# Queries and keys produced feature-major, with their rotary halves swapped by transfers inside SBUF

## The chip, the core and the metric

One decoder layer runs on one core of a Trainium2 chip. The metric is the device time of one execution in microseconds. The kernel before takes 363.92 us (median of three runs, 363.71 to 363.99); the execution that was profiled took 363.52 us, of which 361.7 us is the span from its first to its last instruction.

## What is computed

The layer has 256 positions and width 1024. All products are made in float32 accuracy by splitting each operand into a high and a low part that the matrix engine takes ("h" and "l"), and adding three products: high by high, high by low, low by high.

```
proj  = x @ w_in          # [q 512 | k 512 | v 512 | B 512 | C 512 | h 512 | gates 2048]
q, k  = rotate the first 16 of each head's 64 dimensions   (8 heads)
y_att = softmax(mask(q @ k.T / 8)) @ v @ w_attn_out         # one block of 256 keys, causal
y_cnv = (B * causal_dwconv3(C * h)) @ w_conv_out
mix   = (sigmoid(g_att) * y_att + sigmoid(g_cnv) * y_cnv) @ w_o
x     = LayerNorm(alpha * x + mix)
u     = causal_dwconv3(x @ w_up);  f = (silu(u_gate) * u_val) @ w_down
x     = LayerNorm(alpha * x + f)
```

The rotation takes, per head, dimensions 0 to 7 as x1 and 8 to 15 as x2 and gives x1*cos - x2*sin and x2*cos + x1*sin. The angle is the position times one of eight frequencies.

## The kernel before, in words

The schedule is written out by hand: each engine executes its instructions in the order in which the program issues them. `plan()` cuts all weights into chunks of at most 128 x 2048 numbers, which SP loads in order into three `raw` buffers (`issue_dma`). Each chunk holds units; a unit is split into a high part (`wh`, ScalarE copies with rounding) and a low part (`wl`, VectorE subtracts). There are nine buffers of each. A chunk's buffer is free for the next load when VectorE has made the low part of its last unit.

**The x stage (lines 571 to 629).** Chunks 0 to 7 each hold one block of 128 features of x, transposed, and the rows of `w_in` that belong to it: 512 columns of q, 512 of k, 512 of v. For each block k, `qkv_passes` issues for q, k and v and for each half t of the positions three matmuls of 512 columns (line 596): x is the stationary operand, the weights stream past, and the result is position-major (128 positions by 512 features). Six accumulators collect it over eight blocks: four for q and k in the pool `acc`, two for v in the pool `ps`. The pools have four banks each, taken in rotation. `rope_tables` makes the cosines and sines position-major, 8 numbers per position, in three parts after blocks 2, 3 and 4.

**The stage C0 (lines 545 to 720).** From unit `C0` on, units are made in pairs by `two_units` and `cols_pair`: here the weights are stationary and x streams past, so the result is feature-major (128 features by 256 positions). A *wide* matmul (line 338) streams the high and the low part of x together, 512 columns; a *narrow* one (line 345) streams the high part alone past the low part of the weights, 256 columns. One unit takes 8 of each, over 8 blocks. Order within a pair: 8 wide of the first unit, 8 wide of the second, 8 narrow of the first, 8 narrow of the second. The pairs come as h0, c0, b0, h1, c1, b1 (two halves of h, C and B), then eight pairs of gates g. Each pair takes two `acc` banks, so pair b0 takes over the banks of h0, which VectorE frees with `conv_sum_dve` (line 642).

What else happens in this stage is hung on units by `at(unit, engine part, function)` and issued by `slot(u)`: first the unit's matmuls, then the hung matrix and ScalarE work, then splits of weights four to five units ahead, then hung VectorE work. `rope(t)` (lines 372 to 375, VectorE) rotates q and k position-major at C0 and C0 + 1; `qk_transpose` (line 383) turns them feature-major by 16 matrix-engine transposes at C0 + 2, behind the first unit of pair c0; `qk_h` and `qk_l` (lines 390, 393, 228) split the result into `qkT`. `scores` (line 411) is hung at C0 + 4 for head pairs 0 and 1, and at C0 + 9 for 2 and 3: 20 small matmuls each, behind the first unit of b0 and the second of c1. Masks, softmax, transposes of the probabilities and the products with v follow at later units.

GpSimd has little to do: constants at the start, 128 x 256 additions of masks (line 419) and of outputs, and the loads of the norm parameters.

Of the kernel before, what the change touches and what calls it, by code (L numbers as in the profile page):

```python
# [8 lines left out]
F32 = mybir.dt.float32  # L9
# [6 lines left out]
P = 128  # L16
# [35 lines left out]
PIECES = {0: (0, 768, 1280, 1792), 1: (0, 768, 1792)}  # L52
# [3 lines left out]
LAST = 4  # L56


def plan():
# [80 lines left out]
def layer_kernel(ctx: ExitStack, tc: tile.TileContext, x, wpack, cpack, ln1_g, ln1_b, ln2_g, ln2_b, out):  # L140
# [28 lines left out]
    XR_CHUNK = 20  # L169
# [78 lines left out]

    mask = cst.tile([P, 384], F32, name="mask")
# [14 lines left out]
    invf = cst.tile([P, 8], F32, name="invf")  # L264
    for i, f in enumerate(INV_FREQ):
        nc.gpsimd.memset(invf[:, i:i + 1], f)


    consts = cst.tile([P, 162], F32, name="consts")
    nc.sync.dma_start(consts, cpack)  # L270
    posi = consts[:, 160:162].bitcast(I32)
# [15 lines left out]
    cs = cst.tile([P, 2, 2, 8], F32, name="cs")  # L287

    RT = {}

    def rope_tables(part):

        if part == 2:
            nc.scalar.activation(cs, RT["r"], AF.Sin)
            return
        parts = two_pi_parts(6, 4)
        if part == 1:
            n, r = RT["n"], RT["r"]
            for c in parts[1:]:
                nc.vector.scalar_tensor_tensor(r, n, -c, r, op0=ALU.mult, op1=ALU.add)  # L300
            nc.vector.tensor_scalar(r[:, 0], r[:, 0], math.pi / 2, None, op0=ALU.add)
            nc.vector.tensor_scalar(r, r, PI_LO, -PI_LO, op0=ALU.min, op1=ALU.max)
            return
        posf = cst.tile([P, 2], F32, name="posf")
        nc.vector.tensor_copy(posf, posi)
        ang = cst.tile([P, 2, 8], F32, name="ang")
        nc.vector.tensor_tensor(ang, posf[:, :, None].to_broadcast([P, 2, 8]),
                                invf[:, None, :].to_broadcast([P, 2, 8]), op=ALU.mult)
        n = RT["n"] = cst.tile([P, 2, 2, 8], F32, name="nrev")
        r = RT["r"] = cst.tile([P, 2, 2, 8], F32, name="rrem")  # L310
        for f, ph in ((0, 0.25), (1, 0.0)):
            nc.vector.tensor_scalar(n[:, f], ang, 1.0 / TWO_PI, ph, op0=ALU.mult, op1=ALU.add)
        nc.vector.tensor_scalar(n, n, MAGIC, MAGIC, op0=ALU.add, op1=ALU.subtract)
        for f in range(2):
            nc.vector.scalar_tensor_tensor(r[:, f], n[:, f], -parts[0], ang, op0=ALU.mult, op1=ALU.add)
# [41 lines left out]
    qk = big.tile([P, 2, 2, AW], F32, tag="rows", name="qk")  # L357
# [5 lines left out]
    aT = big.tile([P, 4, 2, S], F32R, tag="d8", name="aT")  # L363
    yT = big.tile([P, 4, 2, S], F32R, tag="e8", name="yT")

    def rope(t):
        xv = qk[:, t].rearrange("p a (h d) -> p (a h) d", d=HD)[:, :, 0:16].rearrange("p h (i f) -> p h i f", i=2)
        a = scratch([P, 16, 2, 8], f"ra{t}")
        b = scratch([P, 16, 2, 8], f"rb{t}")
        co = cs[:, 0, t][:, None, None, :].to_broadcast([P, 16, 2, 8])  # L370
        si = cs[:, 1, t][:, None, None, :].to_broadcast([P, 16, 2, 8])
        nc.vector.tensor_tensor(a, xv, co, op=ALU.mult)
        nc.vector.tensor_tensor(b, xv, si, op=ALU.mult)
        nc.vector.tensor_tensor(xv[:, :, 0, :], a[:, :, 0, :], b[:, :, 1, :], op=ALU.subtract)
        nc.vector.tensor_tensor(xv[:, :, 1, :], a[:, :, 1, :], b[:, :, 0, :], op=ALU.add)

    def qk_transpose(g2):

        b = ps_bank(f"qkt{g2}")
        for gi in range(2):  # L380
            g = 2 * g2 + gi
            for t in range(2):
                nc.tensor.transpose(b[:, gi * 256 + t * P:gi * 256 + (t + 1) * P],
                                    qk[:, t, g // 4, (g % 4) * P:(g % 4 + 1) * P], ident)
        QB[g2] = b.rearrange("p (g t) -> p g t", g=2)
# [3 lines left out]
    def qk_h(g2):  # L389
        nc.scalar.activation(qkT[:, 0, 2 * g2:2 * g2 + 2, :], QB[g2], AF.Copy)  # L390

    def qk_l(g2):
        low(qkT[:, 1, 2 * g2:2 * g2 + 2, :], QB[g2], qkT[:, 0, 2 * g2:2 * g2 + 2, :])
# [3 lines left out]
    def scores(ps):  # L397
# [4 lines left out]
        for t in range(2):  # L402
            n = (t + 1) * P
            for p in ps:
                for a, b in ((0, slice(0, 2)), (1, 0)) if t == 0 else ((0, 0), (0, 1), (1, 0)):
                    for j in range(2):
# [4 lines left out]
                        nc.tensor.matmul(o, qkT[hs, a, p, t * P:(t + 1) * P], qkT[hs, b, 4 + p, 0:n],  # L411
# [81 lines left out]
    def attend_h(p):  # L493
        nc.scalar.activation(aT[:, p, 0, :], PR[p, "c"][:, 0], AF.Copy)
# [40 lines left out]
    def evac_rows(i, banks):  # L535
        for t in range(2):
            nc.scalar.activation(qk[:, t, i, :], banks[t], AF.Copy)

# [6 lines left out]
    C0 = U[(OFF_H, 0)]  # L545
    for t in range(2):
        at(C0 + t, "dve", rope, t)
    for g2 in (0, 2, 1, 3):
        at(C0 + 2, "pe", qk_transpose, g2)
        at(C0 + 3, "act", qk_h, g2)  # L550
        at(C0 + 3, "dve", qk_l, g2)

# [53 lines left out]
    for p in (0, 2):  # L606
        qkv_passes(0, 0, (0, 1), (p,))
# [535 lines left out]
```

## Time and profile before

| what | value |
|---|---|
| median of three runs | 363.92 us |
| the profiled execution | 363.52 us |
| its span | 361.7 us |
| granted TensorE clock, mean | 0.999 |
| moved by DMA | 69.63 MB, 193 GB/s over the span |

In the profile, PE is the matrix engine's matmuls and PEld its weight loads, DVE is VectorE, ACT ScalarE, POOL GpSimd, SP the queue that issues the weight loads. A timeline row gives the start, the length, the engine, the line, the output and inputs, the tile shapes, the count of instructions merged into the row, and in brackets the idle time before it with what ended that. Matmuls overlap, since the next one streams in while the last one drains. So the length of a single matmul is no price; the distance from one start to the next is.

### The profile page before, as it was taken

The page shows a single profiled execution, that of the slowest core. Times are in us where ns is not written, and L with a number is a line of the kernel's source. Part 1 is how long each engine was busy: PE and PEld are TensorE (multiplying, and loading weights), DVE is VectorE, ACT ScalarE, POOL GpSimd, SP SyncE. Part 2 cuts the span into 40 slices and gives each one's busy share as a digit, 9 for nine tenths or more (in the row PEclk, how much of TensorE's full clock was granted, in tenths as well). Part 3 has the DMA queues.
Part 4 walks back from the last instruction along what each step waited for, and adds up shares of the span by engine and source line. Part 5 has one row for each costly group of instructions (what it writes and reads, how often), then busy time and mean ns, then how long its engine had stood idle before and what let it go on. Part 6 is the DMA issues. An engine that isn't in the chain of part 4 may idle for free.

```text
span 361.7 us, 5228 instructions
## 1 busy us (share of the span) xinstructions
PE 355.0 (98%) x1935; PEld 307.0 (85%) x1935; DVE 298.5 (83%) x518; ACT 232.2 (64%) x415; POOL 21.7 (6%) x49
## 2 busy tenths in 40 slices
PE   9999999999999999999999999999999999999993
PEld 8888888888898888888888888888888888888883
DVE  4696887989795969989769888969779697999875
ACT  5576758787977966653357576656757476577800
POOL 2000001000000113301000000000000000000110
PEclk9999999999999999999999999999999999999999
DMA  7988563536653454688160845456281736663011
GB/s 287 337 298 331 169 234 117 216 116 222 245 208 142 134 216 130 250 318 290 61 234 18 332 131 219 146 202 226 125 342 40 316 102 247 232 235 116 3 51 65
DMA packets 11098, 69.63 MB, mean 193 GB/s; under 512 B 1216, under 2 KB 1472, under 8 KB 4032
## 3 DMA queue, kind: packets, MB, share of 16 engines
q1 hardware_dynamic: 10352, 67.00, 50.7%
q0 software_dynamic: 576, 2.10, 1.9%
q8 instruction: 15, 0.25, 0.3%
q10 hardware_dynamic: 144, 0.20, 0.1%
q14 instruction: 11, 0.09, 0.1%
HBM read 68.24 MB, written 1.05 MB: 192 GB/s over the span
## 4 chain that ended last, share of the span: by engine, by line
PE 95%; issue 3%; DVE 1%; POOLq 0%; POOL 0%; DVEq 0%
PE pb L338 20%; PE pb L345 11%; PE g L338 8%; PE d L320 5%; PE d L321 5%; PE d L322 4%; PE g L345 4%; PE y L338 4%; PE q L596 3%; PE k L596 3%; PE v L596 3%; PE b L338 2%; PE y L345 2%; PE c L338 2%; PE o L320 2%
## 5 line engine op out<-in xcount | busy, mean ns | idle before, releaser
L209 DVE TENSOR_TENSOR wl<-raw,wh 128x1024 fp32r<-128x1024 f32 x99 | 121.9, 1233 | 22.1 <-ACT wh L199 21.5
L199 ACT ACTIVATE wh<-raw 128x1024 fp32r<-128x1024 f32 x99 | 103.7, 1054 | 25.9 <-DMA raw<-in_wpack 25.8
L338 PE MATMUL pb<-x1T,wh 128*128 128x512 f32 x320 | 76.2, 390 | 0.0
L338 PEld LDWEIGHTS pb<-x1T,wh 128*128 128x128 f32 x320 | 59.7, 188 | 12.1
L345 PEld LDWEIGHTS pb<-x1T,wl 128*128 128x128 f32 x320 | 41.0, 191 | 1.6
L345 PE MATMUL pb<-x1T,wl 128*128 128x256 f32 x320 | 41.5, 283 | 0.0
L232 DVE TENSOR_TENSOR wl<-raw,wh 128x1024 fp32r<-128x1024 f32 (+1 forms) x29 | 27.3, 982 | 6.1 <-ACT wh L231 5.8
L338 PE MATMUL g<-xT,wh 128*128 128x512 f32 x128 | 31.8, 395 | 0.0
L320 PE MATMUL d<-wh,f 128*128 128x512 f32 x76 | 29.8, 392 | 0.0
L321 PE MATMUL d<-wl,f 128*128 128x512 f32 x76 | 29.8, 391 | 0.0
L322 PE MATMUL d<-wh,f 128*128 128x512 f32 x76 | 29.6, 389 | 0.0
L231 ACT ACTIVATE wh<-raw 128x1024 fp32r<-128x1024 f32 (+1 forms) x29 | 23.7, 859 | 8.1 <-PE o L322 4.0
L338 PEld LDWEIGHTS g<-xT,wh 128*128 128x128 f32 x128 | 23.2, 188 | 4.6
L863 ACT ACTIVATE fb<-pb 128x512 f32<-128x512 f32 x20 | 11.9, 593 | 17.5 <-PE pb L345 17.4
L881 DVE SCALAR_TENSOR_TENSOR fc<-fb,consts,fc 128x254 f32<-128x254 f32 x40 | 19.3, 483 | 1.4
L879 DVE SCALAR_TENSOR_TENSOR fc<-fb,consts,fc 128x255 f32<-128x255 f32 x40 | 19.1, 478 | 0.0
L873 ACT ACTIVATE fc<-fb,consts 128x256 f32<-128x256 f32 x40 | 18.0, 497 | 1.2 <-DVE fb L867 1.1
L345 PEld LDWEIGHTS g<-xT,wl 128*128 128x128 f32 x128 | 16.4, 191 | 0.7
L322 PEld LDWEIGHTS d<-wh,f 128*128 128x128 f32 x76 | 14.3, 188 | 3.1
L345 PE MATMUL g<-xT,wl 128*128 128x256 f32 x128 | 16.6, 282 | 0.0
L320 PEld LDWEIGHTS d<-wh,f 128*128 128x128 f32 x76 | 14.3, 189 | 2.6
L321 PEld LDWEIGHTS d<-wl,f 128*128 128x128 f32 x76 | 14.3, 189 | 2.4
(206 smaller groups left out, 593.8 us busy)
## 6 DMA issues: line engine op xcount, KB each, us to landing
raw<-in_wpack SPq DMA_DIRECT2D x55, 1024.0 KB, 4.9
raw<-in_wpack SPq DMA_DIRECT2D x6, 896.0 KB, 6.6
xr<-in_x SPq DMA_DIRECT2D x1, 1024.0 KB, 7.1
ln<-in_ln_g POOLq DMA_DIRECT2D x2, 512.0 KB, 5.2
ln<-in_ln_b POOLq DMA_DIRECT2D x2, 512.0 KB, 5.8
raw<-in_wpack SPq DMA_DIRECT2D x2, 384.0 KB, 3.9
raw<-in_wpack SPq DMA_DIRECT2D x2, 256.0 KB, 3.5
raw<-in_wpack SPq DMA_DIRECT2D x1, 512.0 KB, 5.6
```

Source lines behind the costliest of these rows:

```text
L199: nc.scalar.activation(units[u]["h"], raw_of(u), AF.Copy)
L209: nc.vector.tensor_tensor(units[u]["l"], raw_of(u), units[u]["h"].bitcast(F32), op=ALU.subtract)
L231: nc.scalar.activation(h, src, AF.Copy)
L232: (eng or nc.vector).tensor_tensor(l, src, h.bitcast(F32), op=ALU.subtract)
L320: nc.tensor.matmul(o, ah, bh, start=start, stop=False)
L321: nc.tensor.matmul(o, ah, bl, start=False, stop=False)
L322: nc.tensor.matmul(o, al, bh, start=False, stop=stop)
L338: nc.tensor.matmul(bank, un["h"][:, k, n0:n0 + P], b[:, k].rearrange("p a s -> p (a s)"), start=k == 0, stop=False)
L345: nc.tensor.matmul(bank[:, 0:S], un["l"][:, k, n0:n0 + P], b[:, k, 0], start=False, stop=k == nk - 1)
L596: nc.tensor.matmul(banks[m][t], (xl if p == 2 else xh)[:, k, t * P:(t + 1) * P], wl if p == 1 else wh, start=k == 0 and p == 0, stop=k == ...
L879: nc.vector.scalar_tensor_tensor(c[:, 1:S], pb[:, a * S:a * S + S - 1], w_ffn(1, j), c[:, 1:S], op0=ALU.mult, op1=ALU.add)
L881: nc.vector.scalar_tensor_tensor(c[:, 2:S], pb[:, a * S:a * S + S - 2], w_ffn(0, j), c[:, 2:S], op0=ALU.mult, op1=ALU.add)
```

## The change

- The q and k weights become eight units of 128 columns, in the order q0 k0 q1 k1 q2 k2 q3 k3. Six of them (`QK = 6`) stand beside v in each chunk of the x stage, which shrinks from 1792 to 1536 columns; the last two (q3, k3) come as an own chunk of two units, at the new mark `qk`, ahead of C0, and are made by `two_units` like every other pair.
- In the x stage, per block: v as before (6 matmuls of 512), then for the six q/k units one wide and one narrow matmul each. v comes first, except in the last block, where it comes last.
- `qk_act` and `qk_dve` add the two halves of each feature-major result into `qk`, as the h, C and B units do. `qk_swap` copies, per group of 64 partitions, eight partitions of `qk` into `swap` by transfers inside SBUF, four transfers of 8 partitions x 1024 numbers for units 0 to 3 and four for units 4 to 7, on SP's queue.
- The rotation is cos * q on VectorE (`rope_cos`), sin * swapped on GpSimd (`rope_sin`), and their sum on VectorE (`rope_sum`), over whole 128 x 512 tiles in which unrotated dimensions have cosine 1 and sine 0. `qk_h` and `qk_l` split the sum from SBUF, not from a PSUM bank.
- The cosines and sines are feature-major, 128 x 256 each. Frequencies come out of a constant tile by one more matrix-engine transpose at the start; positions come by a transfer of their own (`prow`, on GpSimd's queue); the tables are made in five parts after blocks 1 to 5.
- `qk_transpose` and its 16 transposes are gone.
- The two lines that hang `scores` at C0 + 4 and C0 + 9 stand twice in the new text.

```diff
@@ plan
     for k in range(KT):
         chunk((1, S, [("xT", k, k + 1, 0, S)]),
-              (2, 512, [("w_in", k, k + 1, 0, 1024)]),
-              (1, 512, [("w_in", k, k + 1, 1024, 1536)]))
+              (1, AW, [("w_in", k, k + 1, 2 * AW, 3 * AW)]),
+              (QK, P, [("w_in", k, k + 1, qk_col(s), qk_col(s) + P) for s in range(QK)]))
+    mark("qk")
+    chunk(*[(8, P, [("w_in", 0, 8, qk_col(s), qk_col(s) + P)]) for s in (QK, QK + 1)])
@@ constants
+    freqs = tmp.tile([P, P], F32, tag="gs", name="freqs", bufs=3)
+    nc.gpsimd.memset(freqs, 0.0)
+    for h, sign in enumerate((-1.0, 1.0)):
+        for i, f in enumerate(INV_FREQ):
+            nc.gpsimd.memset(freqs.rearrange("p (j d) -> p j d", j=2)[:, :, 8 * h + i:8 * h + i + 1], sign * f)
+    nc.tensor.transpose(warm[:, P:2 * P], freqs, ident)
+    posr = cst.tile([P, S], I32, name="posr")
+    nc.gpsimd.dma_start(posr, bass.AP(tensor=prow.tensor, offset=prow.offset, ap=[[0, P], [1, S]]))
@@ rope_tables, on 128 x 256 tiles
+        if part == 0:
...
+            nc.vector.tensor_copy(posf, posr)
+            nc.vector.tensor_scalar(r, posf, freq[:, 0:1], None, op0=ALU.mult)
+            nc.vector.tensor_scalar(n, r, 1.0 / TWO_PI, None, op0=ALU.mult)
+            nc.vector.tensor_scalar(n, n, MAGIC, MAGIC, op0=ALU.add, op1=ALU.subtract)
+        if part in (0, 1, 2):
+            for c in (parts[0:1], parts[1:4], parts[4:])[part]:
+                nc.vector.scalar_tensor_tensor(r, n, -c, r, op0=ALU.mult, op1=ALU.add)
+        if part == 2:
             nc.vector.tensor_scalar(r, r, PI_LO, -PI_LO, op0=ALU.min, op1=ALU.max)
+        if part == 3:
+            nc.vector.scalar_tensor_tensor(a, r, -1.0, r, op0=ALU.mult, op1=ALU.max)
+            nc.scalar.activation(cs[:, 1], r, AF.Sin)
+            nc.scalar.activation(cs[:, 0], a, AF.Sin, bias=halfpi, scale=-1.0)
+        if part == 4:
+            nc.vector.tensor_scalar(cs[:, 0], cs[:, 0], freq[:, 2:3], freq[:, 1:2], op0=ALU.mult, op1=ALU.add)
+            nc.vector.tensor_scalar(cs[:, 1], cs[:, 1], freq[:, 2:3], None, op0=ALU.mult)
@@ the rotation
+    def qk_act(s, bank):
+        QB[s] = scratch([P, S], f"qb{s}", tag="gs", bufs=3)
+        nc.scalar.activation(QB[s], bank()[:, S:2 * S], AF.Copy)
+    def qk_dve(s, bank):
+        nc.vector.tensor_tensor(qk[:, s], bank()[:, 0:S], QB[s], op=ALU.add)
+    def qk_swap(b):
+        for p in range(0, P, HD):
+            for h in (0, 8):
+                nc.sync.dma_start(swap[p + h:p + h + 8, 4 * b:4 * b + 4], qk[p + 8 - h:p + 16 - h, 4 * b:4 * b + 4])
+    def rope_cos(p):
+        QB["r", p] = scratch([P, 2, S], f"rope{p}")
+        nc.vector.tensor_tensor(QB["r", p], qk[:, 2 * p:2 * p + 2], table(0), op=ALU.mult)
+    def rope_sin(p):
+        nc.gpsimd.tensor_tensor(swap[:, 2 * p:2 * p + 2], swap[:, 2 * p:2 * p + 2], table(1), op=ALU.mult)
+    def rope_sum(p):
+        nc.vector.tensor_tensor(QB["r", p], QB["r", p], swap[:, 2 * p:2 * p + 2], op=ALU.add)
@@ what is hung where
+    S0, C0 = U["qk"], U[(OFF_H, 0)]
+    for p in range(2):
+        at(S0, "dve", rope_cos, p)
+        at(S0, "dve", rope_sin, p)
+        at(S0 + 1, "dve", rope_sum, p)
+        at(C0 + p, "act", qk_act, QK + p, lambda p=p: q3k3[p])
+        at(C0 + p, "dve", qk_dve, QK + p, lambda p=p: q3k3[p])
+    at(C0 + 1, "dve", qk_swap, 1)
+    for p in range(4):
+        if p > 1:
+            at(C0 + p - 1, "dve", rope_cos, p)
+            at(C0 + 2, "dve", rope_sin, p)
+            at(C0 + 3, "dve", rope_sum, p)
+        at(C0 + p // 2 * 4, "act", qk_h, p)
+        at(C0 + p // 2 * 4, "dve", qk_l, p)
+    at(C0 + 4, "pe", scores, (0, 1))
+    at(C0 + 9, "pe", scores, (2, 3))
 
     at(C0 + 4, "pe", scores, (0, 1))
     at(C0 + 9, "pe", scores, (2, 3))
@@ the x stage
+    def qk_passes(k, ss):
+        w = units[U["qkv"] + 3 * k + 2]
+        for s in ss:
+            nc.tensor.matmul(qb[s], w["h"][:, s, :], xT[:, k].rearrange("p a s -> p (a s)"), start=k == 0, stop=False)
+        for s in ss:
+            nc.tensor.matmul(qb[s][:, 0:S], w["l"][:, s, :], xh[:, k], start=False, stop=k == KT - 1)
...
+    q3k3 = two_units(S0, ("q3", "k3"))
```

More of the change, by code (lines that the diff above doesn't have):

```diff
@@ L304, in rope_tables @@
[L304 to L312, printed above, removed]
@@ L377, in qk_transpose @@
[L377 to L385, printed above, removed]
-    QB = {}
[L389 to L393, printed above, removed]
+    QB = {}
@@ L395, in layer_kernel, with qk_l @@
+    def qk_l(p):
+        low(qkT[:, 1, 2 * p:2 * p + 2, :], QB["r", p], qkT[:, 0, 2 * p:2 * p + 2, :])
     SB, SM, PR = {}, {}, {}
@@ L606, in layer_kernel @@
     for p in (0, 2):
-        qkv_passes(0, 0, (0, 1), (p,))
+        v_passes(0, (p,))
     nc.vector.tensor_tensor(wl0[:, 0], w0[:, 0], wh0[:, 0].bitcast(F32), op=ALU.subtract)
-    qkv_passes(0, 0, (0, 1), (1,))
-    split_part(1, 1, 2)
-    qkv_passes(0, 1, (0, 1), (0, 2, 1))
-    split(2)
-    qkv_passes(0, 2, (0, 1), (0, 2, 1))
+    v_passes(0, (1,))
+    split_start(2)
+    for s in (0, 3):
+        split_part(2, s, s + 3)
+        qk_passes(0, range(s, s + 3))
+    rope_freqs()
     qkv_split(1)
```

137 lines of the change are left out of this document (64 added, 73 removed).

## The prediction

> **What bounds the kernel now.** I read the engines' busy times first, then the chain that ended last, then who waits for whom with the filter on the matrix engine.
>
> ```profile
> span 361.7 us, 5228 instructions
> PE 355.0 (98%) x1935; PEld 307.0 (85%) x1935; DVE 298.5 (83%) x518; ACT 232.2 (64%) x415; POOL 21.7 (6%) x49
> PE 95%; issue 3%; DVE 1%; POOLq 0%; POOL 0%; DVEq 0%
> PE warm L245 <- PEq L1133: 0.8, 1, 0.8
> ```
>
> The busy 98% alone proves little, since overlapping matmuls count as busy. The last row does: in the whole span the matmuls wait for nothing but the start of the program. So a matmul added or removed moves the end by its distance to the next one, and any wait that the change puts in front of a matmul is added whole. The question is thus twofold: how much matmul work comes and goes, and whether VectorE, 83% busy, still keeps ahead. The timeline of the matrix engine gives the prices, as distances between starts:
>
> ```profile
> 4.43 1.75 PE L596 MATMUL q<-wh,xT 128*128 128x512 f32 x4
> ...
> 9.21 0.39 PE L596 MATMUL q<-wh,xT 128*128 128x512 f32 x1
> ...
> 33.69 0.39 PE L596 MATMUL q<-wh,xT 128*128 128x512 f32 x1
> ...
> 37.77 3.79 PE L338 MATMUL h<-xT,wh 128*128 128x512 f32 x16
> 41.40 2.08 PE L345 MATMUL h<-xT,wl 128*128 128x256 f32 x16
> 43.31 2.01 PE L338 MATMUL c<-xT,wh 128*128 128x512 f32 x8
> 45.16 1.91 PE L383 MATMUL qkt<-ident,qk 128*128 128x128 f32 x16
> 46.83 2.07 PE L338 MATMUL c<-xT,wh 128*128 128x512 f32 x8
> 48.74 2.08 PE L345 MATMUL c<-xT,wl 128*128 128x256 f32 x16
> 50.65 2.00 PE L338 MATMUL b<-xT,wh 128*128 128x512 f32 x8
> 52.58 1.43 PE L411 MATMUL s<-qkT 64*128 64x256 f32 x20
> 53.95 2.09 PE L338 MATMUL b<-xT,wh 128*128 128x512 f32 x8
> 55.88 2.08 PE L345 MATMUL b<-xT,wl 128*128 128x256 f32 x16
> 57.79 3.82 PE L338 MATMUL h<-xT,wh 128*128 128x512 f32 x16
> ...
> 69.01 1.44 PE L411 MATMUL s<-qkT 64*128 64x256 f32 x20
> 70.38 3.96 PE L338 MATMUL b<-xT,wh 128*128 128x512 f32 x16
> ```
>
> A wide matmul costs (41.40 - 37.77)/16 = 0.227 us, a narrow one (43.31 - 41.40)/16 = 0.119, a clean pair of units 5.54. Block 0 of the x stage takes 4.78 us for 18 matmuls, 0.70 more than 18 x 0.227; the later blocks 4.08 each.
>
> **The change on the matrix engine.** q and k now: 2 x 2 x 3 x 8 = 96 matmuls of 512 columns, 96 x 0.227 = 21.8 us. After: 8 units x 8 blocks, 64 wide and 64 narrow, 14.5 + 7.6 = 22.2. The columns are the same, but a narrow matmul costs more than half a wide one: **+0.4**. v is unchanged.
>
> The 16 transposes go. Pair c takes 50.65 - 43.31 = 7.34 against 5.54 for h, so their worth, with the change of mode around them, is **-1.8** (between -1.7, their own distance 46.83 - 45.16, and -1.8).
>
> The scores double. The new text hangs both calls twice, and nothing takes the first copy out, so 40 small matmuls come on top, each burst right behind its twin. A burst lasts 53.95 - 52.58 = 1.37, and 70.38 - 69.01 = 1.37: **+2.7**. Bounds: by columns alone, 16 x 256 + 4 x 128 shared between two halves of the array, 2304 at 0.227/512, 1.02 a burst, 2.0 in all; above, pair b's full excess, 57.79 - 50.65 - 5.54 = 1.60, twice: 3.2. I take 1.37, since a twin needs no change of mode.
>
> The transpose of the frequencies stands behind the warm-up, ahead of the first block. GpSimd's 17 small fills are done near 2 us, and the first block waits for data until 4.43; it costs nothing, or 0.1 (a transpose's distance) without that cover.
>
> Sum: 0.4 - 1.8 + 2.7 = **+1.3** (0.6 to 1.8).
>
> **The x stage.** A block now asks 6 x 0.227 + 6 x 0.346 = 3.44 us of the matrix engine, not 4.08; its end comes at 4.43 + 0.70 + 8 x 3.44 = 32.65. Can VectorE follow?
>
> ```profile
> 18.24 1.83 DVE L232 TENSOR_TENSOR wl<-raw,wh 128x1024 fp32r<-128x1024 f32 x2 [0.52 <-ACT wh L231]
> 19.98 0.16 DVE L305 CAST posf<-consts 128x2 f32<-128x2 int32 x1
> ...
> 21.14 0.42 DVE L232 TENSOR_TENSOR xT<-raw,xT 128x256 fp32r<-128x256 f32 x1
> ...
> 23.23 1.32 DVE L300 SCALAR_TENSOR_TENSOR rrem<-nrev,rrem 128x32 f32<-128x32 f32 x6
> ...
> 24.89 0.42 DVE L232 TENSOR_TENSOR xT<-raw,xT 128x256 fp32r<-128x256 f32 x1
> ...
> 64.24 1.01 DVE L450 TENSOR_SCALAR sm<-sm,st 128x128 f32<-128x128 f32 x4
> ...
> 66.96 1.92 DVE L658 SCALAR_TENSOR_TENSOR ct<-z,consts,ct 128x256 f32<-128x256 f32 x4
> ...
> 26.67 0.42 ACT L231 ACTIVATE xT<-raw 128x256 fp32r<-128x256 f32 x1 [0.67 <-DMA raw<-in_wpack]
> raw<-in_wpack SPq DMA_DIRECT2D x6, 896.0 KB, 6.6
> ```
>
> The tables cost 1.16 + 1.66 = 2.8 us now (19.98 to 21.14, 23.23 to 24.89). Over 128 x 256 a fused operation takes 1.92/4 = 0.48 and a simple one about 0.3; with some 0.05 where each waits for the last, the five parts are 1.9, 1.6, 1.95, 0.5 and 0.7, **6.6 together**. A block's low parts take about 1.8 (1536 columns in 1.83 now). So three blocks ask 3.4 to 3.75 of VectorE against 3.44. What covers this is its lead: the last block's data lands at 26.67 and is used at 33.69. After, its use comes at 29.2. Smaller chunks land sooner (I take 24.1, from 6.0 us of landing after the release of the buffer, a little under the 6.6 for larger ones), and through VectorE's queue its low parts are ready near 29.1. The lead is used up, no more: 0, bound 2.
>
> **The stage behind it.** With q3/k3 the pairs start at 32.65 (S0), 38.19 (h0), 43.73 (c0) and 49.27 (b0). Pair b0 needs h0's two banks, which VectorE empties.
>
> ```profile
> 39.77 1.23 DVE L209 TENSOR_TENSOR wl<-raw,wh 128x1024 fp32r<-128x1024 f32 x1
> 40.91 0.42 DVE L372 TENSOR_TENSOR ra<-qk,cs 128x256 f32<-128x256 f32 x1
> ...
> 42.11 1.22 DVE L209 TENSOR_TENSOR wl<-raw,wh 128x1024 fp32r<-128x1024 f32 x1
> ...
> 45.58 0.41 DVE L642 TENSOR_TENSOR ch<-h,ch 128x256 f32<-128x256 f32 x1
> 45.91 1.21 DVE L209 TENSOR_TENSOR wl<-raw,wh 128x1024 fp32r<-128x1024 f32 x1
> 47.05 2.47 DVE L228 TENSOR_TENSOR qkT<-qkt,qkT 128x512 fp32r<-128x512 f32 x4
> 49.44 0.41 DVE L642 TENSOR_TENSOR ch<-h,ch 128x256 f32<-128x256 f32 x1
> 55.77 0.74 POOL L419 TENSOR_TENSOR lo<-lo,mask 128x256 f32<-128x256 f32 x1 [0.74 <-ACT lo L418]
> ...
> 56.03 1.56 DVE L209 TENSOR_TENSOR wl<-raw,wh 128x1024 fp32r<-128x1024 f32 x1
> ...
> 0.74 2.27 SPq L177 DMA_DIRECT2D raw<-in_wpack  x5
> out<-x SPq DMA_DIRECT2D x2, 256.0 KB, 2.0
> ```
>
> Now the banks come free at 46 and 50, some 4 us before 50.65 and 53.95. In their place: rotation goes from 2 x 1.2 us (40.91 to 42.11) to eight sums of 0.34, four products and four sums of 0.62 (2.47/4, an operation of that size), 7.7 us, while qkT's lows stay 2.5. Add the tables' 3.8 and VectorE has **9 us more** before pair h1, and only 4 of lead.
>
> Hence its queue, from 29.1: last table part 0.7; four splits of 1.14 for S0 and h0 (4.6), with 0.5 for h0's chunk; six sums 2.0; v 1.25; four more splits 4.6; two products, two sums (0.6 lost on GpSimd), two lows 4.4; q3's and k3's sums 0.7. k3 is summed at **47.7**. Then a product, a split, a product and h0's first bank (0.34): 50.4, where the matrix engine wants it at 49.27, **1.1 late**. The second bank stands behind the last two rotary sums, and these behind a chain that the trace doesn't have yet: four transfers issued at 0.45 each (2.27/5), 1.8, queued on SP behind a weight load that waits for a split just ahead; landing 2.0 (the nearest row; nothing here moves from SBUF to SBUF); two GpSimd products, 128 x 512 at twice 0.74, 2.9; a sum 0.6; the bank 0.4. That is 55.4. The matrix engine reaches it at 49.27 + 1.1 + 1.8 + 2.7 = 54.9, **0.5 late**. Together **+1.6**; 0 if VectorE is 2 us sooner, 4 if 2.4 later. Behind the wait, on the matrix engine's queue, stands everything to the end.
>
> The other four transfers (units 0 to 3) and their products end near 42.9, ahead of the scores at 51; free, unless they slip by 5 us. `prow`'s transfer and the fill of `swap` lie in GpSimd's empty first microseconds. ScalarE's work is as large as now.
>
> A word on GpSimd: at 56.03 a split beside a 0.74 us mask addition took 1.56, not 1.23, so it lost 0.33, some 45% of the addition. [...]
>
> **The forecast.** 363.52 + 1.3 + 1.6 = 366.4 against the profiled execution, which lies 0.4 below the median; on the median, **366.8**.
>
> **Rivals.**
> (1) VectorE keeps ahead. Idle stretches of some 4 us now precede the stage, and data comes sooner; then only matmuls count: 363.9 + 1.3 = 365.2. Against it: 9 us of new work.
> (2) GpSimd's products hold VectorE. By the row 45% of the early 2.9 us, 1.3, falls on the banks: 368.1; excluding each other in full, 2.9: 369.7. For it: the row at 56.03. Against it: part of the time VectorE waits for those products anyway.
> (3) The tables starve the x stage: 2 us before block 7: 368.8. For it: 3.75 against 3.44. Against it: three blocks only, and they begin with a lead.
> (4) Not slower: twin bursts run at the floor by columns, 1.02, since weights and mode are ready; it decides whether the second burst's distance is under 1.1. The sum falls to +0.6, VectorE keeps ahead: 364.5, no change that can be told. Against it: both bursts now take 1.37 though one starts on a delayed weight load.
> That the change doesn't do what it says is in the sum: it takes 16 transposes off the matrix engine and puts 40 score matmuls on.
>
> **Chances.** Forecast 0.35, (1) 0.27, (2) 0.20, (3) 0.10, (4) 0.08. The range 364.9 to 369.8 reaches over (1) to the top of (2) and leaves out (4) and some of the top. About 0.2% (0.7 us) is what can be told from no change: slower 0.87; same 0.10, nearly all of it (4) and the low end of (1); faster 0.03, if (4) comes with a shorter block 0.
>
> **What would show it.** Per step: 80 score matmuls, second bursts of 1.37; no qkt row; pair c at 5.5; first pair behind the x stage at 32.65, and no wait of the matrix engine before it; at b0's two units a wait on VectorE's h sums, 1 us and less. If the waits list stays empty, (1); if a split beside the sin products takes over 2 us, (2); if block 7 waits for `wl`, (3). The forecast is wrong if the time is under 364.9, where the twin bursts would have to cost half, or if the wait lies elsewhere.

## The result, and the profile after

The changed kernel takes 373.58 us in the median of four runs (371.94 to 374.50), beside 363.81 (363.63 to 363.99) for the kernel before on the same chip: 1.0264 times as long, 95% interval 1.0227 to 1.0300. The forecast was 366.8 (364.9 to 369.8). The sign was right, the size was not: 9.8 us more instead of 2.9. The profiled execution is the lowest of the four, 371.94 us.

From the page of the kernel after: the span, the engines' busy times, the chain that ended last by engine.

```profile
span 370.2 us, 5404 instructions
PE 357.3 (97%) x1992; PEld 308.7 (83%) x1992; DVE 310.0 (84%) x531; ACT 233.2 (63%) x422; POOL 31.4 (8%) x65
PE 82%; DVE 6%; issue 4%; DMA 4%; SPq 1%; ACT 1%; POOL 1%; POOLq 0%; DVEq 0%; ACTq 0%
```

The matrix engine's share of the chain fell from 95% to 82%: the chain now runs through VectorE, DMA and GpSimd. Whom the matrix engine waited for, in us in total, times, longest (the 0.8 us at the program's start, there before too, left out):

```profile
PE c L359 <- DVE qk L398: 2.0, 2, 1.4
PE v L633 <- DVE wh L648: 1.7, 1, 1.7
PE b L359 <- DVE ch L695: 1.2, 1, 1.2
PE v L633 <- ACT wh L240: 0.6, 1, 0.6
PE v L633 <- DVE wl L241: 0.2, 1, 0.2
```

Only the third row is a wait that I had forecast. The matrix engine's timeline:

```profile
6.11 1.16 PE L633 MATMUL v<-wh,xT 128*128 128x512 f32 x4 [1.73 <-DVE wh L648]
...
35.29 2.10 PE L359 MATMUL q<-xT,wh 128*128 128x512 f32 x8
...
40.97 3.82 PE L359 MATMUL h<-xT,wh 128*128 128x512 f32 x16
44.62 2.07 PE L366 MATMUL h<-xT,wl 128*128 128x256 f32 x16
48.09 2.11 PE L359 MATMUL c<-xT,wh 128*128 128x512 f32 x8 [1.40 <-DVE qk L398]
50.76 2.11 PE L359 MATMUL c<-xT,wh 128*128 128x512 f32 x8 [0.57 <-DVE qk L398]
52.71 2.08 PE L366 MATMUL c<-xT,wl 128*128 128x256 f32 x16
54.62 2.00 PE L359 MATMUL b<-xT,wh 128*128 128x512 f32 x8
56.56 2.73 PE L441 MATMUL s<-qkT 64*128 64x256 f32 x40
60.45 2.12 PE L359 MATMUL b<-xT,wh 128*128 128x512 f32 x8 [1.15 <-DVE ch L695]
...
75.75 2.73 PE L441 MATMUL s<-qkT 64*128 64x256 f32 x40
78.41 3.92 PE L359 MATMUL b<-xT,wh 128*128 128x512 f32 x16
```

Pair b1 starts at 78.41, 8.03 us later than before (70.38). The forecast for it was 70.38 + 1.3 + 1.6 = 73.28, so 5.13 were missed here, and the rows place them:

| place | forecast | after | more than forecast |
|---|---|---|---|
| end of the x stage (start of S0) | 32.65 | 35.29 | 2.64 |
| pair S0 | 5.54 | 40.97 - 35.29 = 5.68 | 0.14 |
| pair c0, from the end of h0 at 44.62 + 1.91 = 46.53 | 5.54 | 54.62 - 46.53 = 8.09 | 2.55 |
| waits at b0 | 1.6 | 60.45 - 56.56 - 2.7 = 1.19 | -0.41 |

That is 4.92 of the 5.13. Of the 2.64, 1.68 are there at the first matmul (6.11 for 4.43); most of the rest are the waits of block 1, 0.6 and 0.2. In c0 the two waits shown are 1.97; the other 0.58 pass around them, since a wait is counted from the end of the last matmul (44.62 + 2.07 = 46.69, not 46.53).

The last 0.5 us lie behind the last store. It is issued at 358.61 before and at 366.63 after, and from there to the span's end it is 3.1 us before and 3.6 after. All traces of the changed form show 3.5 to 3.6, those of the form before 3.1; why is open.

What VectorE did at the places of the waits (kernel after, timeline):

```profile
3.79 2.17 DVE L648 CAST wh<-raw 128x512 fp32r<-128x512 f32 x1 [3.79 <-DMA raw<-in_wpack]
...
44.20 2.36 DVE L417 TENSOR_TENSOR rope<-rope,swap 128x512 f32<-128x512 f32 x2 [1.19 <-POOL swap L414]
...
47.62 0.41 DVE L398 TENSOR_TENSOR qk<-q,qb 128x256 f32<-128x256 f32 x1
...
50.29 0.41 DVE L398 TENSOR_TENSOR qk<-k,qb 128x256 f32<-128x256 f32 x1
...
57.70 2.36 DVE L417 TENSOR_TENSOR rope<-rope,swap 128x512 f32<-128x512 f32 x2 [3.19 <-POOL swap L414]
59.98 0.41 DVE L695 TENSOR_TENSOR ch<-h,ch 128x256 f32<-128x256 f32 x1
```

GpSimd, and the issues of the swaps on SP's queue, kernel after:

```profile
2.00 0.71 POOL L266 DMA_DIRECT2D posr<-in_prow  x1
...
3.88 1.79 POOL L381 MEMSET swap<- 128x2048 f32 x1
42.12 3.29 POOL L414 TENSOR_TENSOR swap<-swap,cs 128x512 f32<-128x512 f32 x2 [36.45 <-DMA swap<-qk]
56.38 2.52 POOL L414 TENSOR_TENSOR swap<-swap,cs 128x512 f32<-128x512 f32 x2 [10.97 <-DMA swap<-qk]
```

```profile
37.42 2.81 SPq L404 DMA_DIRECT2D swap<-qk  x4
...
50.78 2.67 SPq L404 DMA_DIRECT2D swap<-qk  x4
```

The four products and the four sums that wait for them, count, then shortest, median and longest in ns:

```profile
L414 POOL TENSOR_TENSOR swap<-swap,cs x4: 1278/1286/2041, 42.1 to 57.6; 128x512 f32<-128x512 f32 x4
L417 DVE TENSOR_TENSOR rope<-rope,swap x4: 679/1218/1761, 44.2 to 59.4; 128x512 f32<-128x512 f32 x4
```

Four readings. The first cast of the kernel, 0.43 us before, takes 2.17 and ends at 5.96, 0.29 behind the fill of `swap` (3.88 + 1.79 = 5.67). VectorE stands idle for 1.19 and 3.19 us for GpSimd's products, and each time the sums of banks that the matrix engine is waiting for (47.62 and 50.29 for c0, 59.98 for b0) are queued behind. And the bank that comes first is not h0's: the pool rotates, S0 took the two `acc` banks that c0 wants, so q3's and k3's sums are due at c0's start, 46.53. I had k3's sum at 47.7 and did not compare it with the c0 start that I had, 43.73. And GpSimd and VectorE hold each other up: the first product starts beside a split (41.79 to 43.01) and takes 2.04, not 1.28; the first sum of each pair runs beside the second product and takes 1.76, not 0.68.

The page's table of transfers, over the first 12 us, KB each and us to landing, kernel after:

```profile
raw<-in_wpack SPq DMA_DIRECT2D x3, 384.0 KB, 7.8
```

Before, the transfers of that size in that stretch landed in 3.9 us; they are not the same pieces, since the change cuts the first chunks otherwise.

### The profile page after: what moved, and what is told of

Read it like the earlier page. It is cut to its first block, busy times and chain, and to the rows that moved or that the text cites. A ratio compares the mean times of both kernels' runs of the same rounds, so it can differ in the third digit from the quotient of the medians.

```text
span 370.2 us, 5404 instructions
## 1 busy us (share of the span) xinstructions
PE 357.3 (97%) x1992; PEld 308.7 (83%) x1992; DVE 310.0 (84%) x531; ACT 233.2 (63%) x422; POOL 31.4 (8%) x65
## 4 chain that ended last, share of the span: by engine, by line
PE 82%; DVE 6%; issue 4%; DMA 4%; SPq 1%; ACT 1%; POOL 1%; POOLq 0%; DVEq 0%; ACTq 0%
PE pb L359 20%; PE pb L366 10%; PE g L359 8%; PE d L341 4%; PE d L342 4%; PE d L343 4%; PE g L366 4%; PE y L359 4%; PE y L366 2%; DVE wl L241 2%; DMA raw<-in_wpack 2%; PE o L343 2%; PE o L341 2%; PE o L342 2%; PE b L359 2%
## 5 line engine op out<-in xcount | busy, mean ns | idle before, releaser
L218 DVE TENSOR_TENSOR wl<-raw,wh 128x1024 fp32r<-128x1024 f32 x101 | 123.8, 1227 | 22.5 <-ACT wh L208 22.3
L208 ACT ACTIVATE wh<-raw 128x1024 fp32r<-128x1024 f32 x101 | 105.7, 1053 | 27.5 <-DMA raw<-in_wpack 27.4
L241 DVE TENSOR_TENSOR wl<-raw,wh 128x1024 fp32r<-128x1024 f32 (+3 forms) x29 | 25.2, 907 | 1.8 <-ACT wh L240 1.3
L240 ACT ACTIVATE wh<-raw 128x1024 fp32r<-128x1024 f32 (+3 forms) x29 | 21.9, 800 | 7.2 <-PE o L343 4.0
L1100 POOL TENSOR_TENSOR fs<-fs 128x256 f32<-128x256 f32 (+1 forms) x4 | 2.6, 670 | 169.3 <-ACT fs L1097 169.2
```

The source lines that it names most:

```text
L208: nc.scalar.activation(units[u]["h"], raw_of(u), AF.Copy)
L218: nc.vector.tensor_tensor(units[u]["l"], raw_of(u), units[u]["h"].bitcast(F32), op=ALU.subtract)
L240: nc.scalar.activation(h, src, AF.Copy)
L241: (eng or nc.vector).tensor_tensor(l, src, h.bitcast(F32), op=ALU.subtract)
```

## The experiments

All times are medians beside runs of the kernel before on the same chip (363.7 to 364.0).

### Moving the fill, then the positions, then both

The copy on GpSimd makes both wait until `rope_freqs` has run on VectorE, some 3 us later.

```diff
@@ e2: the fill late; e3: the positions late; e5: both
-    nc.gpsimd.dma_start(posr, ...)
-    nc.gpsimd.memset(swap, 0.0)
...
     rope_freqs()
+    nc.gpsimd.tensor_copy(freq[:, 3:4], freq[:, 2:3])
+    nc.gpsimd.dma_start(posr, ...)
+    nc.gpsimd.memset(swap, 0.0)
```

> The changed kernel with the 128 x 2048 fill of swap on GpSimd put behind a one-column copy that waits for VectorE's work on block 0. Theory A (the fill, 3.88 to 5.67, holds VectorE's first cast, 3.79 to 5.96, and with it the first matmul): the cast takes 0.43 us again, the first matmul starts near 4.5 instead of 6.1 us, and the time falls by 1 to 1.7 us, to about 372. Rival B (the start is late because data lands late, by the transfer of positions and the smaller pieces): the cast still ends near 6 us, or the first matmul starts early but the x stage still ends near 35.3 us: no more than 0.3 us faster.

Measured: 373.38 us (372.50 to 374.01), ratio 1.0260 (1.0233 to 1.0287). The cast took 0.43 again and the first matmul started at 4.40, but the time did not fall. The matrix engine's timeline and the stretch of 2 us that follows (busy us of PE, PEld, DVE, ACT and POOL with their instructions; then the granted clock, the DMA share and GB/s):

```profile
10.44 0.49 PE L632 MATMUL v<-wh,xT 128*128 128x512 f32 x1 [2.03 <-ACT wh L240]
```

```profile
12.00:14.00 2.00, 2.00 (x6) 1.59 (x5) 0.98 (x3) 1.48 (x4) 0.00 (x0) 0.50 0.76 261
```

Block 1's data were as late as in the kernel after, so the 1.7 us won became a wait of 2.03, and behind it the clock fell to 0.50: 6 matmuls in 2 us. The x stage ended at 36.85, even later. The fill was one of two late things.

> The changed kernel with the transfer of positions on GpSimd's queue put behind a one-column copy that waits for VectorE's work on block 0; the fill of swap stays where it is and so starts about 0.7 us sooner. Theory A (the third piece of chunk 0 lands at 7.3 and chunk 1 at 9.4 us, against 4.8 and 6.9 before, because the positions' 128 packets of 1 KB are in front of them): the waits of 0.6 and 0.2 us at block 1 go, chunk 1 lands near 7 us; together with the earlier fill the x stage ends 1 to 1.5 us sooner, near 372.3. Rival B (the smaller pieces themselves land late): the third piece still lands past 6.5 us and block 1 still waits.

Measured: 372.67 us (371.87 to 373.44), ratio 1.0242 (1.0216 to 1.0268). No wait in block 1 any more. The cast now meets a fill that ran from 3.13 to 4.93:

```profile
3.72 1.49 DVE L647 CAST wh<-raw 128x512 fp32r<-128x512 f32 x1 [3.72 <-DMA raw<-in_wpack]
```

It ended at 5.21, again 0.28 behind the fill. The x stage still ended at 35.1: from 5.36 to 9.87 the matrix engine took 4.5 us for what takes 2.5 in the kernel after (6.11 to 8.62), at about half pace, which gave back what the earlier start and data had won. The gain is under what these four runs can tell.

> Fill of swap and transfer of positions both behind the one-column copy. Theory A (the start has two independent causes, the fill that holds the first cast and the positions that hold chunk 1's data, and each alone leaves the matrix engine idle for some 2 us, after which the granted clock falls to 0.5 for about 4 us): only with both moved does the x stage run through: first matmul at 4.4, chunk 1 landing near 7, no granted clock under 0.9, x stage ending near 32.7 to 33 us instead of 35.3. The waits at c0 and b0 stay, so 370 to 371 us. Rival B (the smaller pieces or the extra splits limit the x stage in any case): it still ends past 34.5 us.

Measured: 371.30 us (369.51 to 373.71), ratio 1.0209 (1.0156 to 1.0261). The x stage is mended: first matmul at 4.46, and no wait in it but 0.23. Its transfers over the first 12 us, beside the 7.8 above:

```profile
raw<-in_wpack SPq DMA_DIRECT2D x3, 384.0 KB, 5.3
```

With the positions alone moved (e3) it was 5.6, with the fill alone (e2) 7.8 as before. In all eleven traces of the changed form it is 7.8 to 8.7 where the positions are sent at the start and 5.0 to 5.7 where they are sent later. So the 128 KB of positions, sent to all partitions at 2.00, had delayed the weights behind them by 2.2 to 2.5 us. But the time fell by only some 2 us, for the matrix engine ran into the next wait:

```profile
34.77 3.48 PE L358 MATMUL q<-xT,wh 128*128 128x512 f32 x8 [1.79 <-DVE qk L396]
```

S0 waits for the sums of the x stage's own banks, and its eight matmuls take 3.28 us (to the next row at 38.05) where 1.9 are usual: the clock was 0.78 and 0.50 in the stretches from 34 to 38. VectorE was late there because the data were. What it waited for from 30 to 62 us:

```profile
DVE wl L241 <- ACT wh L240: 1.6, 2, 1.3
```

These are splits of the next units' weights, which stand ahead of the sums; ScalarE had waited 1.77 us for their transfer. This changes from one execution to the next: of the five kernels with this same x stage, the weight chunks of 1024 KB issued between 15 and 33 us land in 4.7 to 4.9 us in e6, e7 and e12, which wait at S0 for 0.8 us at most, and in 6.8 and 7.1 in e5 and e9, which wait for 1.79 and 2.34. Why they land at different speeds no run shows.

### A fill in the kernel before

```diff
@@ e10, in the kernel before, behind the constants
+    fill = big.tile([P, KT, S], F32, tag="d8", name="fill")
+    nc.gpsimd.memset(fill[:, 0:5], 0.0)
+    nc.gpsimd.memset(fill, 0.0)
```

> The kernel before, with nothing added but two fills of a tile with zeros on GpSimd behind its constants (128 x 1280, then 128 x 2048, the latter from about 3.8 to 5.6 us; nothing reads the tile). Theory A (a fill on GpSimd holds VectorE's one-input cast for as long as it lasts): the cast takes about 2 us in place of 0.43, the first matmul starts near 6 us, and the time rises by 1.6 us, or by up to 3.5 if the granted clock falls after the idle. Rival B (the cast was late for another reason, its data or the positions' transfer): cast 0.43 us and the time within 0.3 us of before.

Measured: 364.56 us (363.52 to 366.19), ratio 1.0031 (1.0013 to 1.0048). Four of ten runs lie at 366.0 to 366.2, the others at 363.5 to 364.6. In the profiled one, which is of the second kind, the cast was not held (VectorE, then GpSimd):

```profile
3.64 0.44 DVE L607 CAST wh<-raw 128x512 fp32r<-128x512 f32 x1 [3.64 <-DMA raw<-in_wpack]
```

```profile
2.64 1.16 POOL L268 MEMSET fill<- 128x1280 f32 x1
3.86 1.97 POOL L269 MEMSET fill<- 128x2048 f32 x1
```

The data had come 0.1 to 0.2 us sooner than in most other traces, and the cast fell on the seam between the two fills: it began 0.16 ahead of the recorded end of the first (2.64 + 1.16 = 3.80) and was not held by that. Two groups about 2 us apart are what a cast that sometimes gets ahead of the second fill would give, but no trace shows the slower one. This experiment does not settle the fill's price; that the fill holds the cast is shown by e2 and e3.

### The bank sums ahead of the rotary sums

```diff
@@ e4
-        at(S0 + 1, "dve", rope_sum, p)
...
     at(C0 + 1, "dve", qk_swap, 1)
+    for p in range(2):
+        at(C0 + 1, "dve", rope_sum, p)
...
-        at(C0 + p // 2 * 4, "act", qk_h, p)
-        at(C0 + p // 2 * 4, "dve", qk_l, p)
+        at(C0 + 2 + p // 2 * 2, "act", qk_h, p)
+        at(C0 + 2 + p // 2 * 2, "dve", qk_l, p)
```

> The changed kernel with the first two rotary sums and their splits hung behind the sums of q3 and k3 (from S0 + 1 and C0 to C0 + 1 and C0 + 2). Theory A (pair c0 waits for the banks of q3 and k3, whose sums stand on VectorE behind rotary sums that wait for the transfers and for GpSimd; it is the order, not the amount): the waits at c0 (1.4 and 0.6 us) go, the second four transfers start 3 to 4 us sooner and the wait at b0 shrinks: 2.5 to 3.5 us faster, 370 to 371. Rival B (VectorE has 9 us more work than it has time for, whatever the order): the waits move to b0 and h1 and the time falls by less than 1 us.

Measured: 370.53 us (370.07 to 370.88), ratio 1.0183 (1.0161 to 1.0205): 3 us less, with no operation less. Whom the matrix engine waited for:

```profile
PE v L634 <- DVE wh L649: 1.8, 1, 1.8
PE q L359 <- DVE qk L398: 0.6, 1, 0.6
PE b L359 <- DVE ch L696: 0.6, 2, 0.4
```

The row of c0 is gone, and b0's shrank by half; the late start is as it was. From S0 to b1 the profiled executions take 40.33 us here (36.99 to 77.32) and 43.12 in the kernel after. The order in which VectorE is made to wait was worth over twice the +1.3 that the change puts on the matrix engine on balance.

### The scores hung once

```diff
@@ e1
-    at(C0 + 4, "pe", scores, (0, 1))
-    at(C0 + 9, "pe", scores, (2, 3))
```

> The changed kernel with each call of scores hung once. Theory A (the matrix engine is the bound only where nothing waits; in the changed kernel the second unit of b0 waits 1.15 us for h0's second bank right behind the doubled burst): of the 2 x 1.33 us of extra matmuls the first lies in that wait, so the wait grows to about 2.5 us and only the second burst is saved: 1.3 to 1.5 us faster than the changed kernel, some 372.2 us. Rival B (as the prediction priced it, all of the extra matmuls count): 2.7 us faster, 370.9 us, with the wait at b0 unchanged.

Measured: 374.69 us (372.12 to 375.21), ratio 1.0283 (1.0233 to 1.0334). Nothing was won, which neither theory had; the runs overlap with those of the kernel after. The matrix engine at b0, and a stretch of 2 us there:

```profile
62.60 2.92 PE L359 MATMUL b<-xT,wh 128*128 128x512 f32 x8 [2.80 <-DVE ch L692]
65.32 2.84 PE L366 MATMUL b<-xT,wl 128*128 128x256 f32 x16
```

```profile
64.00:66.00 2.00, 2.00 (x8) 1.66 (x7) 2.00 (x4) 1.98 (x8) 0.98 (x1) 0.50 0.00 0
```

Without the twin the wait at b0 is 2.80, not 1.15: the matrix engine came sooner to a bank that came no sooner. Then the clock fell to half: from 62.60 to h1 at 68.00 are 5.40 us, where the kernel after takes 64.31 - 60.45 = 3.86. Those 1.5 us eat up the second burst, whose twin did go. Doing less work, the engine idled longer (2.80 us) and then ran at a clock of 0.50. The rest of this execution's delay is not the edit's: it starts S0 at 37.10, 1.8 later than the kernel after, behind a wait of 1.4 that lies ahead of the scores.

### The scores hung twice in the kernel before

```diff
@@ e11
     at(C0 + 4, "pe", scores, (0, 1))
     at(C0 + 9, "pe", scores, (2, 3))
+    at(C0 + 4, "pe", scores, (0, 1))
+    at(C0 + 9, "pe", scores, (2, 3))
```

> The kernel before, with the two lines that hang scores standing twice and nothing else changed. Theory A (where the matrix engine never waits, each extra burst costs its own 1.33 us): 2.7 us more than before, 366.5 us, with no wait of the matrix engine. Rival B (the bursts are cheaper behind their twin, at the 1.02 of their columns): 2.0 us. Rival C (the masks' later start makes VectorE late elsewhere): over 3.2 us, with waits.

Measured: 366.37 us (365.87 to 366.71), ratio 1.0073 (1.0060 to 1.0086), 2.7 more than the kernel before. The matrix engine:

```profile
52.69 2.73 PE L411 MATMUL s<-qkT 64*128 64x256 f32 x40
55.35 2.10 PE L338 MATMUL b<-xT,wh 128*128 128x512 f32 x8
```

A double burst takes 2.66, 1.29 more than a single one (1.37). Where the matrix engine waits for nothing, the term of the prediction stands.

### Putting them together

e6 is e5 with e4's order, e7 is e6 with the scores hung once.

> Both late, and the first rotary sums behind the sums of q3 and k3. Theory A: the x stage's 2.5 us and the 3 us of the order add up: 366 to 367 us, no wait of the matrix engine over 0.7 us behind the x stage. What is left over the kernel before is then the matrix work alone, the +1.3 of the prediction and about 1 of small waits. Rival B (VectorE sets the pace of the stage): the faster x stage only makes the waits at S0, c0 and b0 longer, and the time stays at 369 or above.

> As e6, with each call of scores hung once. Theory A (an extra burst costs its 1.33 us where the matrix engine is not waiting, and nothing where it is): with the waits gone it is worth its price now, 2 to 2.7 us less than e6, 363.5 to 364.5 us, level with the kernel before. Rival B (VectorE frees h0's second bank so late that the first burst is still hidden): only 1.3 us less than e6, and a wait of over 1 us at b0.

Measured: e6 368.91 us (367.75 to 369.48), ratio 1.0135 (1.0096 to 1.0175); e7 365.88 (365.33 to 367.19), 1.0064 (1.0041 to 1.0088). e6 lies between its two theories, at the edge of the second. In e7 the x stage ends at 32.85 and the clock stays at full; b1 starts at 72.22. By the medians the twin is worth 3.0 us now, more than theory A had. The traces show less: from S0 to b1 e6 takes 40.64 us (34.47 to 75.11) and e7 39.37, 1.3 less, as rival B had it, since the wait at b0's second unit grew from 0.24 to 1.54 and took the first burst's worth. The other 1.6 between these two executions lie ahead of the edit, in the start of S0. What the medians' 3.0 hold of that, no run separates. Whom the matrix engine waits for in e7, and VectorE and GpSimd in the stretch before:

```profile
PE b L358 <- DVE ch L694: 2.2, 2, 1.5
```

```profile
39.37 3.45 DVE L218 TENSOR_TENSOR wl<-raw,wh 128x1024 fp32r<-128x1024 f32 x2
...
43.08 1.99 DVE L218 TENSOR_TENSOR wl<-raw,wh 128x1024 fp32r<-128x1024 f32 x1
```

```profile
39.75 4.24 POOL L412 TENSOR_TENSOR swap<-swap,cs 128x512 f32<-128x512 f32 x2 [30.21 <-DMA swap<-qk]
```

Two splits take 3.45 beside GpSimd's products, not 2.3, and a third 1.99, not 1.2; the products take 4.24, not the 2.52 of the second pair in the kernel after, beside which no split ran. So both lengthened, the three splits by 1.9 us together and the two products by 1.7; by what means, no run shows.

### Which of VectorE's work is to come first

e8 puts h0's splits behind the x stage's later sums; e9 puts h0's bank sums first and the last rotary sums one unit later; both start from e7.

```diff
@@ e8, in the last block of the x stage
-                if s in (0, 2):
-                    split(S0 + 2 + s // 2)
+                if s in (2, 4):
+                    split(S0 + 1 + s // 2)
@@ e9
-            at(C0 + 3, "dve", rope_sum, p)
+            at(C0 + 4, "dve", rope_sum, p)
-        at(C0 + 2 + p // 2 * 2, "act", qk_h, p)
-        at(C0 + 2 + p // 2 * 2, "dve", qk_l, p)
+        at(C0 + 2 + p // 2 * 3, "act", qk_h, p)
+        at(C0 + 2 + p // 2 * 3, "dve", qk_l, p)
...
-                at(U[(off, pr)] + e + 2, "dve", conv_sum_dve, nm, pr, e)
+                (at_once if (nm, pr) == ("h", 0) else at)(U[(off, pr)] + e + 2, "dve", conv_sum_dve, nm, pr, e)
```

> As e7, with the splits of h0's two units issued behind the sums of q/k units 0 and 1 and of units 2 and 3 in the last block, not ahead of them. Theory A (in e1 and e4 the first unit behind the x stage waited 1.4 and 0.6 us for a q/k bank, since VectorE's sums stood behind a split whose chunk lands late): that wait goes, 0.3 to 0.8 us less than e7. Rival B (the sums then are early, but the split is late for h0 or the wait is hidden): within 0.2 us of e7.

> As e7, with the sums that free h0's banks put ahead of the other work hung on their units, and the last two rotary sums and their splits one unit later. Theory A (what is left of VectorE's lateness, 0.7 and 1.5 us of waits at b0 in e7, is again the order: the sum that frees h0's second bank stands behind rotary sums that wait for transfers and GpSimd): both waits go, 2 us less than e7, 363.4 to 364.0 us. Then the transposes, 1.8 us less matrix work, only pay for what the rest costs, and the time is within 0.2% of the kernel before. Rival B (VectorE is short of time): the waits move to h1 or c1 and the time stays above 365.

Measured: e8 366.88 us (364.62 to 368.77), ratio 1.0078 (1.0049 to 1.0107), no better than e7 within their scatter, with 2.6 us of waits at b0. e9 368.05 (366.17 to 369.56), 1.0106 (1.0086 to 1.0126), worse by the median. Its profiled execution is the slowest of the six, 369.56. Whom the matrix engine waited for there:

```profile
PE q L358 <- DVE qk L396: 2.3, 1, 2.3
PE h L358 <- DVE cc L694: 1.9, 1, 1.9
```

The first row is the wait at S0 for late chunks, ahead of the edit. b0's waits are gone and stand at h1 instead, nearly as long as before, and behind the wait at h1 the clock fell to 0.50 (66 to 68), so that e9 takes 40.65 us from S0 to b1 (35.29 to 75.94) and e7 39.37. Order had been worth 3 us in e4, where VectorE idled; here it only moves the wait. In e7 VectorE still idled for 1.18 us at the last products; in e9 it has no idle time from 33.7 us to h1, but a split beside these products takes 1.97 and the last two sums 2.92, not 1.2 and 1.28.

### The sine products on VectorE

So the shortage is VectorE's time, and the products on GpSimd take some of it where they run beside it (1.9 us in e7). e12 is e7 with the four products on VectorE.

```diff
@@ e12
     def rope_sin(p):
-        nc.gpsimd.tensor_tensor(swap[:, 2 * p:2 * p + 2], swap[:, 2 * p:2 * p + 2], table(1), op=ALU.mult)
+        nc.vector.tensor_tensor(swap[:, 2 * p:2 * p + 2], swap[:, 2 * p:2 * p + 2], table(1), op=ALU.mult)
@@
-        at(S0, "dve", rope_sin, p)
...
+        at(C0 + 1, "dve", rope_sin, p)
         at(C0 + 1, "dve", rope_sum, p)
...
-            at(C0 + 2, "dve", rope_sin, p)
+            at(C0 + 3, "dve", rope_sin, p)
             at(C0 + 3, "dve", rope_sum, p)
```

> The four sine products go from GpSimd to VectorE, each just ahead of its sum; otherwise as in the kernel with both starts late, sums first and the scores once (365.88 us, b0's two units waited 1.5 and 0.7 us). Theory A: GpSimd's products cost more than they carry, since the splits beside them took 3.45 us for two and 1.99 for one where 2.3 and 1.2 are usual, and the last sums waited 1.2 us for them. On VectorE they cost 4 x 0.6 = 2.4 us of its time; 2.0 come back from the splits and the last two sums no longer wait. b0's waits fall from 2.2 us to about 1 and the time to 364 to 365. Theory B: VectorE has no time left and a product costs it its full length; b0's waits grow by up to 2.4, to about 4, and the time to 367 to 369 (more if the clock falls after the longer wait). In both, splits beside the first bank sums take 1.2 us each again.

Measured: 364.87 us (363.84 to 367.77), ratio 1.0054 (1.0030 to 1.0078). Its profiled execution, 364.87 too, waits at b0 for 0.9 instead of 2.2 and takes 38.05 us from S0 to b1 (33.27 to 71.32), e7 39.37. The waits at b0 and VectorE's two splits:

```profile
PE b L358 <- DVE ch L694: 0.9, 2, 0.6
```

```profile
39.79 2.35 DVE L218 TENSOR_TENSOR wl<-raw,wh 128x1024 fp32r<-128x1024 f32 x2
```

The splits are back to 2.35 for two. Four products of 0.7 us on the engine that was short of time shortened the wait, as theory A had it. The runs of e7 and e12 overlap, so that the gain of 1 us rests more on the traces than on the medians. It is the best of the changed kernels by its median, and still 0.3% to 0.8% slower than the kernel before.

## Why the prediction was right in sign and wrong in size

- **The matrix engine's sum, +1.3: right.** The double bursts take 2.66 in the kernel after too, the transposes are gone, a narrow matmul still costs 0.119 (52.71 to 54.62, 16 of them). e11 measured the largest term by itself, 2.7. Rival (4) is out.
- **"Six narrow and six wide a block, 3.44 us": right, and VectorE keeps up there.** With a clean start (e7) the x stage ended at 32.85; forecast 32.65. Rival (3), the tables starving it, is out: no block waits for `wl` but for 0.2 us.
- **"`prow`'s transfer and the fill of `swap` lie in GpSimd's empty first microseconds": the step that failed first.** GpSimd was idle there, but neither work is GpSimd's alone. The fill held VectorE's first cast for 1.7 us, and the transfer of the positions delayed the weights behind it, by 2.2 to 2.5 (e3, e5). I priced an engine's idle time and not what its instruction holds up elsewhere. Measured: 2.64 us at the end of the x stage. That took both edits to mend (e2, e3, e5).
- **"k3 is summed at 47.7 ... 1.1 late, 0.5 late", +1.6: right in mechanism, at the wrong bank and too small.** (The terms add up to 47.85, not 47.7.) VectorE was the one that was late, but "Pair b0 needs h0's two banks" was the only debt that I compared. The first late bank is c0's, and my own queue had it: c0 at 43.73 against q3's sum near 47.3 is 3.6 late, and b0, then at 52.9, would have found its banks free. With 3.6 for 1.6 the sum gives 368.4 for the profiled execution; the waits measured 2.55 at c0 and 1.19 at b0, 3.7. The kernel's lateness in this stage was thus in the terms, and the comparison was missing. k3's sum came when I had it, counted from S0 (50.29 - 35.29 = 15.0, forecast 47.7 - 32.65 = 15.05), but partly by luck: VectorE began this queue 0.9 us sooner (30.80, 4.5 ahead of S0, not 3.55) and lost 1.19 + 1.08 us at the first products, not 0.6. The chain to the second bank was longer than I had it in its issues, 0.7 each and not 0.45 (2.81/4), and in its landing, 2.9 and not 2.0 (53.45 to 56.38). e4, in which the banks' sums no longer stand behind the first rotary sums, took off 3.
- **Rival (2), GpSimd's products holding the splits: not the splits in the kernel after, but the sums.** The split that ran as they began took its usual 1.22, and the product beside it 2.04 for 1.28. Each first sum was held by the second product, 1.76 for 0.68. In e7, with VectorE on time, the splits were held too, for 1.9 us. "Excluding each other in full", from which I had 369.7, was an assumption that no run shows; measured is that this first product lost 0.76 beside a split that lost nothing, and each first sum 1.08. How much of the waits at c0 and b0 in the kernel after is due to this, no run separates.
- **What no step had:** the clock, and how far the landing of the chunks varies. A wait costs its length, and in e1, e2, e4, e5 and e9 one of 1.79 to 2.80 us cost half of the next 3.4 us on top; another of 2.34 in e9 did not. In the profiled execution of the kernel after the clock stays at full after each wait, so the 8.4 us accounted above hold none of it. The other three runs are 1.5 to 2.6 us longer than this one, and none of them was traced. A halved clock as in e1 and e4 would give that, but by my estimate (half of 3.4 us in some 370) it takes 0.005 off the mean granted clock, and theirs are 0.996, 0.992 and 0.998 beside 0.994 here, which speaks against it in two of them, though that column misses some slow matmuls. Chunks that land late, as in e5 and e9, would give it too. It stays open.

What remains of the loss in e12, 1.2 us by the medians and 1.4 between the profiled executions, is not a loss of the idea's matrix work, which by itself saves 1.4 there (0.4 - 1.8). Against that stand the half microsecond at the end, S0 at 33.27 and not 32.65, 0.9 of waits at b0, and some 0.8 in small gaps around them.

## What to carry to other kernels

Before pricing an instruction at nothing because its engine is idle, ask what else it holds up: another engine's instruction beside it, the transfers behind it, what is due behind it in a queue. When a chain through another engine and a transfer is added, list every buffer whose release stands behind it on the waiting engine's queue, in the order in which the pools hand the buffers out, and put the releases ahead. A fix of one lateness shows its worth only when the next one is fixed too; e1, e2 and e3 alone moved the median by 1.1 us at most, and together with e4's edit took off 7.7 (e7). And before a difference of traces is put down to an edit, look whether it begins ahead of the edit, as the waits at S0 in e1 and e9 do.

## What the runs showed of the hardware

- **The clock after a wait.** Of the matrix engine's waits beyond the warm-up, those from 1.37 to 1.67 us (nine of them in seven traces, the start apart) left the granted clock at full; those of 1.79 (e5), 1.93 (e9), 2.03 (e2) and 2.80 us (e1) were followed by a halved clock, in each for the same time: what the stretches of 2 us lose adds up to some 3.4 us at 0.50 (e5: 0.78, 0.50, 0.86 from 34 to 40). One of 2.34 (e9) was not. At the start a wait of 1.73 was not followed by it in the kernel after, and one of 1.81 was in e4. In e1 and e3, after waits of 1.43 and 0.69, the first matmuls ran at half pace (four in 2.05 us, not 1.16) though the profile shows the full clock there, so that column doesn't show everything. A wait's length alone did not decide it, since 1.79 us was followed by a halved clock and 2.34 was not; what did, no run shows.
- **A fill against a cast.** In four traces (e3, the kernel after, e4, e1), whatever the cast's start (3.72, 3.79, 3.81, 3.88), it ended 0.28 to 0.29 us behind the end of GpSimd's fill. Beside no fill it took 0.43 (e2), here 1.49 to 2.17. What decides whether a cast is held, the rows don't tell: in the kernel after it is recorded 0.09 us ahead of the fill, and was held; in e10 it is recorded 0.16 us ahead of the end of one fill, and was not.
- **Small transfers inside SBUF.** Eight partitions by 4 KB took 0.7 us each to issue on SP in the kernel after (2.81 and 2.67 for four), and the first product began 1.9 and 2.9 us behind the end of the issues (40.23 to 42.12, 53.45 to 56.38).
